# Instance norm with a gain, one core: from 32 units of 4 MB to 14 units of 8 MB between 4 small ones

## The chip, the core and the metric

The kernel runs on one core of one Trainium2 chip. The core has TensorE (PE) for matrix products, VectorE (DVE), ScalarE (ACT) and GpSimd (POOL) for elementwise work, SyncE (SP) that here only issues transfers, an on-chip memory (SBUF) of 128 partitions, and 16 DMA engines that move data between it and the device's memory (HBM). SP and ACT each feed a hardware queue of DMAs, in the profile q1 (SP) and q10 (ACT); POOL feeds q0. All three queues run on the same 16 engines.

The metric is the time of one execution on the device in microseconds (us). The kernel before took 627.33 us, the median of 3 runs (626.69 to 627.43).

## The reference

The input is x of shape 4 x 8 x 16 x 256 x 256 in 32-bit floats, which is 512 channels of 65,536 numbers (256 KB each, 134.2 MB in all), and gamma of 8 x 16 numbers. Each channel is normalized by its own mean and variance and scaled by the gamma of its place in the batch:

```python
mu = x.mean(axis=(3, 4), keepdims=True)
var = ((x - mu) ** 2).mean(axis=(3, 4), keepdims=True)
x_norm = (x - mu) / np.sqrt(var + 1e-5)
out = x_norm * gamma[None, :, :, None, None]
```

Every number has to be read once and written once: 134.2 MB each way.

## The kernel before

The 512 channels are cut into `U` = 32 units of 16 channels. A channel lies on `S` = 8 partitions with `F` = 8,192 numbers each, so that a unit fills 128 partitions with rows of 32 KB and is one contiguous piece of 4.19 MB in HBM. `AHEAD` = 6 slots (`xt0` to `xt5`, 192 KB of a partition together) take the units in turn; a unit is loaded into its slot, normalized in place and stored from there.

Before the loop, line 53 and 54 write a small zeroed tile `touch` to the output through POOL, line 55 loads gamma as one row, and six loads are issued (L48), units 1 and 3 through ACT's queue, the others through SP's. VectorE executes 60 instructions that do nothing. POOL makes `navg` (L67 to L72), a block matrix that holds -1/65536 where row and column belong to the same channel. Gamma's row is copied out eightfold into `g_rep` (L83), turned into columns by eight small matmuls (L88; 16 PE instructions in the profile, as each 32-bit matmul is two) and copied to `g_col` (L94): column n holds, on each partition, the gamma of the channel that lies there in unit n, n + 8 and so on.

The loop runs over the units, each engine in the order of the code:

- DVE sums the rows (L107), ACT squares them and sums the squares beside it (L108; its elementwise output `junk` is thrown away), into two columns of `st`.
- PE multiplies `st` by `navg` (L116). `ps` then holds, on all eight partitions of a channel, the negative mean and the negative mean of the squares.
- DVE makes the negative variance `nvar` (L117), ACT takes the root with 1e-5 added (L121), DVE the reciprocal (L125) and the product with gamma (L127).
- DVE subtracts the mean and multiplies, in place, over the whole tile (L130).
- ACT issues the store (L134), and SP issues the load of unit u + 6 into the same slot (L48), which waits until that store has landed.

What sets the order around the change are these two queues: SP's loads stand in line behind one another, each waiting for the store of the unit six before it; ACT's stores stand in line in its queue.

Of the kernel before, what the change touches and what calls it, by code (L numbers as in the profile page):

```python
# [1 line left out]

# [4 lines left out]

F32 = mybir.dt.float32
U8 = mybir.dt.uint8
ALU = mybir.AluOpType  # L10
ACTF = mybir.ActivationFunctionType
AX = mybir.AxisListType


@with_exitstack
def kernel(
    ctx: ExitStack,
    tc: tile.TileContext,
    x: bass.AP,
    gamma: bass.AP,  # L20
    out: bass.AP,
):
    nc = tc.nc
    B, G, C, H, W = x.shape
    P = nc.NUM_PARTITIONS
    HW = H * W
    n_ch = B * G * C
    S = 8
    K = P // S
    F = HW // S  # L30
    U = n_ch // K
    NG = (G * C) // K
    AHEAD = 6
    assert HW % S == 0 and (G * C) % K == 0

    xv = x.rearrange("b g c h w -> (b g c h w)").rearrange("(u p f) -> u p f", p=P, f=F)
    ov = out.rearrange("b g c h w -> (b g c h w)").rearrange("(u p f) -> u p f", p=P, f=F)
    gv = gamma.rearrange("g c -> (g c)")

    data = ctx.enter_context(tc.tile_pool(name="data", bufs=1))  # L40
    singles = ctx.enter_context(tc.tile_pool(name="singles", bufs=1))
    psum = ctx.enter_context(tc.tile_pool(name="psum", bufs=4, space=bass.MemoryType.PSUM))
    ctx.enter_context(tc.manual_schedule())

    slots = [data.tile([P, F], F32, name=f"xt{i}") for i in range(AHEAD)]

    def load(u, queue):
        queue.dma_start(out=slots[u % AHEAD][:], in_=xv[u])  # L48


    g_row = singles.tile([1, G * C], F32, name="g_row")
    touch = singles.tile([16, 128], F32, name="touch")
    nc.vector.memset(touch[:], 0.0)  # L53
    nc.gpsimd.dma_start(out=ov[0][0::S, 0:128], in_=touch[:])  # L54
    nc.gpsimd.dma_start(out=g_row[:], in_=gv[None, :])  # L55
    for u in range(AHEAD):
        load(u, nc.scalar if u in (1, 3) else nc.sync)

    for _ in range(60):
        nc.vector.nop()  # L60

    eps_t = singles.tile([P, 1], F32, name="eps_t")
    nc.gpsimd.memset(eps_t[:], 1e-5)
    one = singles.tile([1, 1], F32, name="one")
    nc.gpsimd.memset(one[:], 1.0)
    navg = singles.tile([P, K, S], F32, name="navg")
    nc.gpsimd.memset(navg[:], -1.0 / HW)  # L67
    nc.gpsimd.affine_select(  # L68
        out=navg[:], in_=navg[:], pattern=[[-S, K], [0, S]], compare_op=ALU.is_ge,
        fill=0.0, base=0, channel_multiplier=1,  # L70
    )
    nc.gpsimd.affine_select(  # L72
        out=navg[:], in_=navg[:], pattern=[[S, K], [0, S]], compare_op=ALU.is_ge,
        fill=0.0, base=S - 1, channel_multiplier=-1,
    )
    navg_w = navg[:].rearrange("p k s -> p (k s)")
    root_eps = singles.tile([P, 1], F32, name="root_eps")
    nc.scalar.activation(out=root_eps[:], in_=eps_t[:], func=ACTF.Sqrt)  # L78
    g_rep = singles.tile([1, NG, K, S], F32, name="g_rep")
    g_ps = psum.tile([P, NG], F32, name="g_ps", bufs=1)  # L80
    g_col = singles.tile([P, NG], F32, name="g_col")

    nc.vector.tensor_copy(  # L83
        out=g_rep[:],
        in_=g_row[:].rearrange("o (n k) -> o n k", n=NG).unsqueeze(3).to_broadcast([1, NG, K, S]),
    )
    for n in range(NG):
        nc.tensor.matmul(  # L88
            out=g_ps[:, n : n + 1],
            lhsT=g_rep[:, n].rearrange("o k s -> o (k s)"),  # L90
            rhs=one[:],
            start=True, stop=True,
        )
    nc.vector.tensor_copy(out=g_col[:], in_=g_ps[:])  # L94

    junk = singles.tile([P, F], U8, name="junk")

    st = singles.tile([P, U, 2], F32, name="st")
    nvar = singles.tile([P, U], F32, name="nvar")
    std = singles.tile([P, U], F32, name="std")  # L100
    rstd = singles.tile([P, U], F32, name="rstd")
    scale = singles.tile([P, U], F32, name="scale")

    squares = []
    for u in range(U):
        t = slots[u % AHEAD]
        nc.vector.reduce_sum(out=st[:, u, 0:1], in_=t[:], axis=AX.X)  # L107
        square = nc.scalar.activation(  # L108
            out=junk[:], in_=t[:], func=ACTF.Square, accum_out=st[:, u, 1:2],
        )  # L110
        if u:

            tc.declare_no_dep(square.ins, squares[-1].ins, reason="junk, ordered by the root between")
        squares.append(square)
        ps = psum.tile([P, 2], F32, name="ps")
        nc.tensor.matmul(out=ps[:], lhsT=navg_w, rhs=st[:, u], start=True, stop=True)  # L116
        nc.vector.tensor_scalar(  # L117
            out=nvar[:, u : u + 1], in0=ps[:, 0:1], scalar1=ps[:, 0:1],
            scalar2=ps[:, 1:2], op0=ALU.mult, op1=ALU.add,
        )  # L120
        nc.scalar.activation(  # L121
            out=std[:, u : u + 1], in_=nvar[:, u : u + 1], func=ACTF.Sqrt,
            bias=eps_t[:], scale=-1.0,
        )
        nc.vector.reciprocal(out=rstd[:, u : u + 1], in_=std[:, u : u + 1])  # L125
        g = u % NG
        nc.vector.tensor_mul(  # L127
            out=scale[:, u : u + 1], in0=rstd[:, u : u + 1], in1=g_col[:, g : g + 1],
        )
        nc.vector.tensor_scalar(  # L130
            out=t[:], in0=t[:], scalar1=ps[:, 0:1], scalar2=scale[:, u : u + 1],
            op0=ALU.add, op1=ALU.mult,
        )
        nc.scalar.dma_start(out=ov[u], in_=t[:])  # L134
        if u + AHEAD < U:
            load(u + AHEAD, nc.sync)


# [1 line left out]
_INS = ['x', 'gamma']  # L140
_OUTS = [((4, 8, 16, 256, 256), 'float32')]


# [23 lines left out]
```

## Time and profile before

| What | Value |
|---|---|
| median of 3 runs | 627.33 us (626.69 to 627.43) |
| span of the profiled execution | 625.8 us |
| DVE busy | 443.4 us, 71% |
| ACT busy | 238.8 us, 38% |
| HBM read, written | 134.22 MB, 134.23 MB |
| mean rate over the span | 429 GB/s |
| reduce of one unit (L107) | 8.684 us |
| squares of one unit (L108) | 7.030 us |
| multiply of one unit (L130) | 4.550 us |

The page of the profile gives for its own execution the span, from the first instruction to the last. Its part 2 cuts the span into 40 slices of 15.6 us and gives the busy share of each engine in tenths. The waits name who waited for whom; the chain follows the work that ended last back to its start; the issues list, for each transfer, the time from its issue to its landing. The trace also holds a record of each packet that a DMA engine moved, with its queue, start, duration and size. A few numbers are from these packet records, and the text says where.

### The profile page before, as it was taken

To read this page: it belongs to the slowest core of one execution; us is meant where nothing else is said; L and a number is where in the kernel's file an instruction comes from. 1 tells how busy PE (TensorE), PEld (TensorE's weight loads), DVE (VectorE), ACT (ScalarE), POOL (GpSimd) and SP (SyncE) were. 2 spreads that over 40 slices of the span, in tenths; PEclk is the share of its full clock that TensorE was granted. 3 is DMA by queue.
4 is the path that set the end of the run, shared out by engine and by line. 5 is a ranking of instruction groups with operands and counts; after the bars stand their busy time and mean duration, and the time that the engine had idled before them with its cause. 6 is when DMAs were issued, how large, how long until landed. Compare 5 with 4: busy or idle time off the path is not lost.

```text
span 625.8 us, 631 instructions
## 1 busy us (share of the span) xinstructions
PE 21.4 (3%) x80; PEld 19.5 (3%) x80; DVE 443.4 (71%) x163; ACT 238.8 (38%) x98; POOL 2.4 (0%) x11
## 2 busy tenths in 40 slices
PE   0200000000000000000000000000000000000000
PEld 0200000000000000000000000000000000000000
DVE  0588999999776687766776667867668676686730
ACT  0444444444443244432344423444224442244400
POOL 1000000000000000000000000000000000000000
DMA  8999999999999999999999999999999999999998
GB/s 369 436 415 429 429 436 436 436 436 434 424 434 434 434 436 434 431 429 434 436 436 436 436 431 427 431 436 431 436 434 434 429 434 436 436 436 436 429 425 354
DMA packets 9282, 268.46 MB, mean 429 GB/s; under 512 B 1072, under 2 KB 1088, under 8 KB 1088
## 3 DMA queue, kind: packets, MB, share of 16 engines
q10 hardware_dynamic: 4896, 142.61, 52.9%
q1 hardware_dynamic: 4320, 125.83, 46.7%
q0 software_dynamic: 64, 0.01, 0.0%
q14 instruction: 2, 0.02, 0.0%
HBM read 134.22 MB, written 134.23 MB: 429 GB/s over the span
## 4 chain that ended last, share of the span: by engine, by line
another core or an unknown queue 61%; DMA 17%; DVE 15%; SPq 1%; PE 1%; issue 0%; ACT 0%
DVE st L107 10%; DMA xt<-in_x_dram 10%; DMA out_dram<-xt 8%; DVE xt L130 5%; SPq L48 1%; PE ps L116 1%; ACT std L121 0%; DVE nvar L117 0%; DVE rstd L125 0%; DVE scale L127 0%
## 5 line engine op out<-in xcount | busy, mean ns | idle before, releaser
L107 DVE TENSOR_REDUCE st<-xt 128x1 f32<-128x8192 f32 x32 | 277.9, 8684 | 101.2 <-DMA xt<-in_x_dram 101.2
L108 ACT ACTIVATE junk<-xt 128x8192 uint8<-128x8192 f32 x32 | 225.0, 7030 | 276.0 <-DMA xt<-in_x_dram 232.8
L130 DVE TENSOR_SCALAR xt<-xt,ps,scale 128x8192 f32<-128x8192 f32 x32 | 145.6, 4550 | 1.2
L121 ACT ACTIVATE std<-nvar,eps_t 128x1 f32<-128x1 f32 x32 | 9.4, 294 | 79.6 <-DVE nvar L117 79.6
L116 PE MATMUL ps<-st,navg 128*128 128x2 f32 x64 | 17.9, 349 | 558.0 <-DVE st L107 558.0
L116 PEld LDWEIGHTS ps<-st,navg 128*128 128x128 f32 x64 | 16.0, 311 | 559.8 <-issue 559.8
L117 DVE TENSOR_SCALAR nvar<-ps 128x1 f32<-128x1 f32 x32 | 9.2, 287 | 23.8 <-PE ps L116 23.8
L125 DVE RECIPROCAL rstd<-std 128x1 f32<-128x1 f32 x32 | 5.2, 164 | 11.6 <-ACT std L121 11.6
L83 DVE COPY g_rep<-g_row 1x1024 f32<-1x1024 f32 x1 | 0.7, 680 | 14.3 <-DMA g_row<-in_gamma_dram 14.3
L108 ACT ACTIVATION_READ_ACCUMULATOR junk<-xt 128x1 f32 x32 | 6.0, 187 | 0.0
L127 DVE TENSOR_TENSOR scale<-rstd,g_col 128x1 f32<-128x1 f32 x32 | 5.1, 159 | 1.1
L88 PE MATMUL g_ps<-one,g_rep 1*128 1x1 f32 x16 | 3.5, 346 | 16.2 <-DVE g_rep L83 16.2
L88 PEld LDWEIGHTS g_ps<-one,g_rep 1*128 1x128 f32 x16 | 3.5, 325 | 16.1 <-issue 16.1
L94 DVE COPY g_col<-g_ps 128x8 f32<-128x8 f32 x1 | 0.2, 166 | 3.7 <-PE g_ps L88 3.7
L78 ACT ACT_TABLE_LOAD x1 | 1.3, 1283 | 1.7 <-PEq L151 1.7
L53 DVE MEMSET touch<- 16x128 f32 x1 | 0.2, 165 | 0.9 <-PEq L151 0.9
L54 POOL DMA_DIRECT2D out_dram<-touch x1 | 0.6, 619 | 0.8 <-DVE touch L53 0.8
L55 POOL DMA_DIRECT2D g_row<-in_gamma_dram x1 | 0.5, 487 | 0.0
L68 POOL TENSOR_SCALAR_AFFINE_SELECT navg<-navg 128x128 f32<-128x128 f32 x1 | 0.4, 400 | 0.1
L72 POOL TENSOR_SCALAR_AFFINE_SELECT navg<-navg 128x128 f32<-128x128 f32 x1 | 0.4, 399 | 0.1
L67 POOL MEMSET navg<- 128x128 f32 x1 | 0.2, 232 | 0.0
L78 ACT ACTIVATE root_eps<-eps_t 128x1 f32<-128x1 f32 x1 | 0.2, 202 | 0.0
(6 smaller groups left out, 0.6 us busy)
## 6 DMA issues: line engine op xcount, KB each, us to landing
out_dram<-xt ACTq DMA_DIRECT2D x32, 4096.0 KB, 62.5
xt<-in_x_dram SPq DMA_DIRECT2D x30, 4096.0 KB, 38.5
xt<-in_x_dram ACTq DMA_DIRECT2D x2, 4096.0 KB, 31.6
out_dram<-touch POOLq DMA_DIRECT2D x1, 8.0 KB, 9.1
g_row<-in_gamma_dram POOLq DMA_DIRECT2D x1, 0.5 KB, 13.3
```

Of the source, the lines that this page charges most:

```text
L48: queue.dma_start(out=slots[u % AHEAD][:], in_=xv[u])
L78: nc.scalar.activation(out=root_eps[:], in_=eps_t[:], func=ACTF.Sqrt)
L83: nc.vector.tensor_copy(out=g_rep[:], in_=g_row[:].rearrange("o (n k) -> o n k", n=NG).unsqueeze(3).to_broadcast([1, NG, K, S]),)
L88: nc.tensor.matmul(out=g_ps[:, n : n + 1], lhsT=g_rep[:, n].rearrange("o k s -> o (k s)"), rhs=one[:], start=True, stop=True,)
L107: nc.vector.reduce_sum(out=st[:, u, 0:1], in_=t[:], axis=AX.X)
L108: square = nc.scalar.activation(out=junk[:], in_=t[:], func=ACTF.Square, accum_out=st[:, u, 1:2],)
L116: nc.tensor.matmul(out=ps[:], lhsT=navg_w, rhs=st[:, u], start=True, stop=True)
L117: nc.vector.tensor_scalar(out=nvar[:, u : u + 1], in0=ps[:, 0:1], scalar1=ps[:, 0:1], scalar2=ps[:, 1:2], op0=ALU.mult, op1=ALU.add,)
L121: nc.scalar.activation(out=std[:, u : u + 1], in_=nvar[:, u : u + 1], func=ACTF.Sqrt, bias=eps_t[:], scale=-1.0,)
L125: nc.vector.reciprocal(out=rstd[:, u : u + 1], in_=std[:, u : u + 1])
L127: nc.vector.tensor_mul(out=scale[:, u : u + 1], in0=rstd[:, u : u + 1], in1=g_col[:, g : g + 1],)
L130: nc.vector.tensor_scalar(out=t[:], in0=t[:], scalar1=ps[:, 0:1], scalar2=scale[:, u : u + 1], op0=ALU.add, op1=ALU.mult,)
```

## The change

Units now come in two sizes. The first two and the last two are as before (16 channels on 8 partitions each, 4.19 MB). The 28 units between are joined to 14 of 32 channels on 4 partitions each, with rows of 64 KB, 8.39 MB a unit. There are three slots of 64 KB a partition, so that the slots take the same 192 KB. Units 0 and 1 share slot 0, one half each, and so do the last two, 16 and 17; units 2 to 15 take the slots 1, 2, 0 in turn.

- A large unit is summed by one instruction and squared by two, of 8,192 numbers each, as `junk` keeps its size; `st` has three columns for it. PE multiplies all three at once. `nvar` takes in the first half's squares, and a new instruction makes the bias `rest` of the root from the second half's.
- There are two block matrices, `navg8` and `navg4`, by a new function `blocks`.
- Gamma is loaded as a tile of 32 partitions x 4 numbers and turned into columns by three matmuls with 0/1 matrices (`pick8a`, `pick8b`, `pick4`), also made by `blocks`. `gamma_of` picks the column of a unit.
- The `touch` write and the 60 idle instructions of DVE are gone. All loads go through SP's queue: four before the loop (units 0 to 3), unit 4 after unit 1, then in the turn of unit u the load of unit u + 3. In the turn of unit 13 the loads of 16 and 17 are issued; in the turn of unit 14, u + 3 is 17, and the load of unit 17 is issued there as well. The program built from it has 19 loads and 18 stores on the two hardware queues. The last load waits for the one before it, into the same bytes, and unit 17's reduce and squares wait for the last.

The core of the diff:

```diff
-    S = 8
-    K = P // S
-    F = HW // S
-    U = n_ch // K
-    NG = (G * C) // K
-    AHEAD = 6
+    GC = G * C
+    SLOTS = 3
+    FS = HW // 8
+    FB = HW // 4
+    KB, KS = P // 4, P // 8
...
-    slots = [data.tile([P, F], F32, name=f"xt{i}") for i in range(AHEAD)]
+    slots = [data.tile([P, FB], F32, name=f"xt{i}") for i in range(SLOTS)]
+    units = []
+    first = 0
+    turn = 0
+    def small(pair):
+        nonlocal first, turn
+        for h in range(2):
+            units.append((first, 8, slots[turn % SLOTS][:, h * FS : (h + 1) * FS]))
+            first += KS
+        turn += 1
+    small(0)
+    while first < n_ch - KB:
+        units.append((first, 4, slots[turn % SLOTS][:]))
+        first += KB
+        turn += 1
+    small(1)
+    U = len(units)
...
+    def load(u):
+        nc.sync.dma_start(out=units[u][2], in_=rows(flat_x, u))
...
-    touch = singles.tile([16, 128], F32, name="touch")
-    nc.vector.memset(touch[:], 0.0)
-    nc.gpsimd.dma_start(out=ov[0][0::S, 0:128], in_=touch[:])
-    nc.gpsimd.dma_start(out=g_row[:], in_=gv[None, :])
-    for u in range(AHEAD):
-        load(u, nc.scalar if u in (1, 3) else nc.sync)
-    for _ in range(60):
-        nc.vector.nop()
+    for u in range(4):
+        load(u)
+    with nc.allow_non_contiguous_dma(reason="128 numbers"):
+        nc.gpsimd.dma_start(out=g_kn[:], in_=gamma.rearrange("g c -> (g c)").rearrange("(n k) -> k n", k=KB))
...
+    def blocks(name, rows_, k, s, value, base):
+        t = singles.tile([rows_, k, P // k], F32, name=name)
+        nc.gpsimd.memset(t[:], value)
+        nc.gpsimd.affine_select(
+            out=t[:], in_=t[:], pattern=[[-s, k], [0, P // k]], compare_op=ALU.is_ge,
+            fill=0.0, base=-base, channel_multiplier=1,
+        )
+        nc.gpsimd.affine_select(
+            out=t[:], in_=t[:], pattern=[[s, k], [0, P // k]], compare_op=ALU.is_ge,
+            fill=0.0, base=s - 1 + base, channel_multiplier=-1,
+        )
+        return t[:].rearrange("p k s -> p (k s)")
+    navg = {8: blocks("navg8", P, KS, 8, -1.0 / HW, 0), 4: blocks("navg4", P, KB, 4, -1.0 / HW, 0)}
...
+    for i in range(3):
+        nc.tensor.matmul(out=g_ps[:, i], lhsT=pick[i], rhs=g_kn[:], start=True, stop=True)
     nc.vector.tensor_copy(out=g_col[:], in_=g_ps[:])
...
     for u in range(U):
...
+        for h in range(parts):
+            square = nc.scalar.activation(
+                out=junk[:], in_=t[:, h * FS : (h + 1) * FS], func=ACTF.Square,
+                accum_out=st[:, u, 1 + h : 2 + h],
+            )
...
+        bias = eps_t[:]
+        if parts == 2:
+            bias = rest[:, u : u + 1]
+            nc.vector.tensor_scalar(
+                out=bias, in0=ps[:, 2:3], scalar1=-1.0, scalar2=1e-5, op0=ALU.mult, op1=ALU.add,
+            )
...
-        nc.scalar.dma_start(out=ov[u], in_=t[:])
-        if u + AHEAD < U:
-            load(u + AHEAD, nc.sync)
+        nc.scalar.dma_start(out=rows(flat_o, u), in_=t)
+        if u == 1:
+            load(4)
+        elif 2 <= u and u + 3 < U:
+            load(u + 3)
+            if u + 3 == U - 2:
+                load(U - 1)
```

## The prediction

> **What bounds the kernel now.** I read the page's slices first, then its queues and DMA issues, the windows, the waits of SP's queue and the chain. The slices show DMA engines that are never free, beside a DVE that idles 29% of the span:
>
> ```profile
> span 625.8 us, 631 instructions
> PE 21.4 (3%) x80; PEld 19.5 (3%) x80; DVE 443.4 (71%) x163; ACT 238.8 (38%) x98; POOL 2.4 (0%) x11
> DMA  8999999999999999999999999999999999999998
> q10 hardware_dynamic: 4896, 142.61, 52.9%
> q1 hardware_dynamic: 4320, 125.83, 46.7%
> ```
>
> The queues carry 34 + 30 = 64 transfers of 4.19 MB, each of 128 rows of 32 KB (and 16 completion packets). What one costs is in the windows (last column GB/s):
>
> ```profile
> 200.00:300.00 100.00, 2.78 (x10) 2.50 (x10) 72.53 (x26) 40.38 (x16) 0.00 (x0) 1.00 1.00 433
> 300.00:400.00 100.00, 2.80 (x10) 2.51 (x10) 72.42 (x26) 39.89 (x17) 0.00 (x0) 1.00 1.00 433
> ```
>
> 4.19 MB at 433 GB/s is 9.68 us: I call this one transfer. 64 of them are 619.6, and the first data move 1.8 into the span (packet records), so an even stream would end at 621.4; the span is 4.4 longer (slower first packets, engines that end up to 1.3 apart, the last landing). I carry these 4.4 over. The median of the runs (627.33) is 1.5 above the profiled span; I carry that too.
>
> SP's waits (in total, times, longest) say that loads wait for stores to free their slot, so the transfers feed each other:
>
> ```profile
> SPq L48 <- DMA out_dram<-xt: 535.3, 26, 59.6
> ```
>
> What covers the last unit is seen in the chain (start, duration) and in the issues (last column: us to landing):
>
> ```profile
> 547.61 38.49 DMA xt<-in_x_dram
> 586.12 8.70 DVE st L107
> 594.95 0.57 PE ps L116 x2
> 596.59 4.55 DVE xt L130
> ```
>
> ```profile
> out_dram<-xt ACTq DMA_DIRECT2D x32, 4096.0 KB, 62.5
> xt<-in_x_dram SPq DMA_DIRECT2D x30, 4096.0 KB, 38.5
> out_dram<-touch POOLq DMA_DIRECT2D x1, 8.0 KB, 9.1
> g_row<-in_gamma_dram POOLq DMA_DIRECT2D x1, 0.5 KB, 13.3
> ```
>
> The last load lands at 586.1 and its unit is ready 15.0 later, at 601.1. The span ends at 625.8, because stores wait 62.5 us in ACT's queue: four of them (38.7 us) are still to move when the last load ends. So the 15 us of arithmetic cost nothing. The small POOL rows show how queues share an engine: 512 bytes of gamma take 13.3 us. By the packet records each small packet starts 2.43 us after the one before it, the time of two 32 KB rows (1.213 each): a row is not cut, and each queue gets one packet per turn, whatever its size.
>
> **The change, part by part.**
>
> *Traffic.* Reading the loop's last lines: at u = 13, `load(16)` is followed by `load(U - 1)`, that is 17; at u = 14 the condition `u + 3 < U` still holds, and `load(17)` is issued again. So there are 19 loads (5 of 4.19 MB, 14 of 8.39) for 18 stores: 33 transfers read, 32 written, 65 in all. One more costs 9.68 us on engines that have no free time. It waits on SP until the first load of 17 has landed (same bytes); nothing is queued behind it there, but unit 17's reduce and squares wait for it.
>
> *Joined DMAs.* 56 of the 64 transfers become 28, SP and ACT issue fewer. An issue takes 0.33 us on a queue that runs ahead: nothing either way. A 64 KB row could cost as much as two 32 KB rows (2 x 1.213) or save one packet's fixed part; nearest row for that part is a 4-byte completion packet, 9 ns: 4 packets x 56 x 9 ns = 2.0 us gained at most. I take 0, since eight rows at 1.213 already make a transfer, and keep 2.0 for the range. The Trainium skill (DMA: Bandwidth & Descriptors, Anatomy of one DMA) puts a DMA at 2.0 us plus bytes at 436 GB/s; 28 fixed parts less would be an estimated 56 us saved if they stood in line. This trace has no such part: a transfer every 9.68 us, queued behind one another.
>
> *Units of 8 MB.* Reduce 2 x 8.68, matmul 0.57, `nvar` 0.30, the new `rest` about 0.3 (as `nvar`, one column), root 0.30, reciprocal and product 0.34, multiply 2 x 4.55, gaps 0.3: 28.5 us, against a pair of 8.39 MB transfers in 38.7. ACT's two squares, 2 x 7.2, end before the reduce does. 18 units take fewer small instructions than 32, but DVE is not what is waited for: 0.
>
> *Three slots.* A slot must go round in 3 x 38.7 = 116.2 us. Its needs: load 38.7 and store 38.7 (both sharing), 28.5, and some 4.3 for starts and landings (1.0 from issue to data, 1.55 from the last data of a load to DVE's start, 0.7 for a store to SP): 110.2. It fits with 6 to spare, and if it did not, the other queue would take the whole rate: DMA stands still only when all three slots are in arithmetic. 0 in the steady part. But the backlog of stores in ACT's queue shrinks from three or four transfers to one being written, and that was the cover of the end.
>
> *Head.* All first loads now go through SP, 25 MB back to back until 60 us, as before. The 128 single numbers of gamma are 8 packets an engine and a completion, one turn each: against one queue of 32 KB rows 9 x 1.21 = 10.9 after a start at about 6, so 17 us; `g_col`'s copy stands before unit 0's reduce on DVE, which so starts near 18 and not at 13. Unit 2 lands near 48 and finds DVE free by 48: 0. If a turn is 2.4, gamma lands near 30 and one or two gaps of 1.7 to 2.6 us open near 80 and 120: 5 us is the upper end. POOL's fifteen small instructions for the five matrices (0.23 to 0.40 each) end near 8 us. The pauses on DVE, the `touch` DMA and the sixteen gamma matmuls (3.5 us) all lay under the first load (22.6): 0.
>
> *The end, which decides.* I play the schedule forward from these rows, one packet per queue and turn. Load 15 ends its data near 546.5, store 14 having begun 5 us before. The small loads 16, 17, 17 again have rows of 32 KB, the stores 14 and 15 rows of 64 KB: a load gets a third of the engine. Load 16 ends near 573 (store 14 done at 571.6). Load 17 runs alone until unit 15 is stored from 577.6, then at a third: 592.6 to 597. Its repeat starts some 2.6 later (landing, issue), at a third against store 15, evenly against store 16 (32 KB rows): 618 to 620. Stores 15 and 16 end at 621.4. Then nothing is left to move: 1.55 landing, 15.0 arithmetic, 1.0 to the first packet, and only at 635.6 to 637.6 does store 17 begin. DMA idles 14 to 16 us.
>
> Sum: 635.6 to 637.6 + 9.68 = 645.3 to 647.3; + 4.4 = 649.7 to 651.7 span; + 1.5 = 651.2 to 653.2. I say **652.0**, that is 9.7 for the repeated load and about 15 for the uncovered end.
>
> **Rivals.**
> *Even shares.* If a 64 KB row is carried as two packets, or engines share by bytes, loads get a half: load 17 ends near 585, its repeat near 607, with 14 us of stores left to cover the 17.6 of landing, arithmetic and start. The idle time is 3.2 us: 624.6 + 9.68 + 4.4 + 1.5 = 640.2. For it: the trace has no row over 32 KB. Against it: a 4-byte packet waited a full turn of two rows.
>
> *64 KB rows move worse.* Neighbouring rows in HBM stand 64 KB apart and not 32. The nearest row of a lower rate is the window 20:40, reads alone: 423 GB/s against 433. Were the 56 joined transfers slower by that 2.3%, 12.5 us more, 664.5. No row has such a pitch, and the first packets had other reasons to be slow. The Trainium skill (DMA: Bandwidth & Descriptors, Latency and other measured facts) speaks against the change here: a row pitch of 512 KiB gave 207 GB/s a direction where 214 is full, 2 MiB 164; 64 KB is below its smallest, and no run here shows any of it. By that 3.3% the estimate would be 18 us more.
>
> *Not slower.* The mechanism would be in the steady part: long rows moving faster. To pay for 25 us, the 56 joined transfers would have to take 9.24 us and not 9.68, 454 GB/s. The bound above is 2.0 us; packets already follow each other with no gap (eight of 1.213 are 9.70). It would also be no slower if the repeat were not issued at all; then by the same schedule 64 transfers and 0 to 3 us without work, 627 to 630, no change or hardly one. The code issues it.
>
> **How the numbers follow.** By turns 0.70 (646 to 658), even shares 0.17 (636 to 645), slower rows 0.08 (658 to 670), not slower 0.05. The range takes the first and nearly all of the second: 638 to 658, about 0.83. Its likeliest part is 647 to 657. About 0.2% (1.3 us) is what a measurement of this kernel can tell from no change. Faster 0.03, same 0.02, slower 0.95.
>
> **What would show it.** 19 loads beside 18 stores, 137 MB read or more (138.4 against 134.2); a DMA digit that drops to 0 once, in the last but one or two slices, for 14 to 16 us (3 with even shares); a last load issued near 594 to 598 that lands near 620 (608); unit 17's reduce starting there, and a chain that ends in load, reduce, multiply, store; 433 GB/s in the middle. Wrong would be: gaps in the middle (three slots too few), another rate in 200:500 (row size matters), or a first unit on DVE after 30 us with holes near 80.

## The result, and the profile after

The changed kernel takes 653.3 us (652.8 to 655.1, 4 runs) against 627.4 of the kernel before: ratio 1.0423, 95% interval 1.0407 to 1.0438, 25.9 us slower. 652.0 was forecast. The profiled execution has a span of 651.6 us, 1.8 below its own time of 653.4. Runs more than 1.5% above the fastest run of their kernel are left out of all ratios.

The page after, its first part, slices, queues and traffic:

```profile
span 651.6 us, 434 instructions
PE 11.5 (2%) x42; PEld 10.4 (2%) x42; DVE 429.4 (66%) x105; ACT 234.7 (36%) x84; POOL 6.2 (1%) x21
DMA  8999999999999999999999999999999999999926
...
q1 hardware_dynamic: 2736, 138.41, 49.4%
q10 hardware_dynamic: 2592, 134.22, 47.6%
...
HBM read 138.41 MB, written 134.22 MB: 418 GB/s over the span
```

The 434 instructions are some two thirds of 631, and this bought nothing: at 66% busy, DVE is not what bounds the kernel. 138.41 MB read are 4.19 more than the input has, the second load of unit 17. And the DMA row, nines until then, has a hole in its last two slices. The windows show how wide it is, and that the middle is as it was (last column GB/s):

```profile
300.00:400.00 100.00, 1.12 (x4) 1.01 (x4) 65.48 (x14) 33.86 (x11) 0.00 (x0) 1.00 1.00 435
400.00:500.00 100.00, 1.67 (x6) 1.50 (x6) 74.92 (x18) 38.84 (x15) 0.00 (x0) 1.00 1.00 435
600.00:620.00 20.00, 0.00 (x0) 0.00 (x0) 0.00 (x0) 0.00 (x0) 0.00 (x0) 1.00 1.01 429
626.00:640.00 14.00, 0.56 (x2) 0.50 (x2) 12.27 (x5) 5.84 (x3) 0.00 (x0) 1.00 0.00 0
```

From 626 to 640 the DMA engines start nothing, while one unit goes through DVE. The end of the chain (start, duration) tells why:

```profile
545.90 53.68 another core or an unknown queue
599.58 0.02 issue
599.60 24.80 DMA xt<-in_x_dram
624.40 0.02 issue
624.42 8.70 DVE st L128
...
634.89 4.55 DVE xt L159
```

SP waits 53.68 us for the first load of unit 17. The chain does not know it by name; SP's waits do:

```profile
SPq L70 <- DMA xt<-in_x_dram: 53.7, 1, 53.7
```

The repeat is issued at 599.6 and lands at 624.4. The last packet of the stores before it ends at 626.5, by the packet records, and store 17 is issued at 639.48 and starts to move at 640.32: 13.8 us in which no data move. In the kernel before, the last unit went through the same 15 us of arithmetic (586.1 to 601.2) while the three stores ahead of its own were moving, until 614.4 by the packet records.

### The profile page after: what moved, and what is told of

The parts are those of the page before. It is cut to its first block, busy times and chain, and to the rows that moved or that the text cites. A ratio compares the mean times of both kernels' runs of the same rounds, so it can differ in the third digit from the quotient of the medians.

```text
span 651.6 us, 434 instructions
## 1 busy us (share of the span) xinstructions
PE 11.5 (2%) x42; PEld 10.4 (2%) x42; DVE 429.4 (66%) x105; ACT 234.7 (36%) x84; POOL 6.2 (1%) x21
## 3 DMA queue, kind: packets, MB, share of 16 engines
q1 hardware_dynamic: 2736, 138.41, 49.4%
HBM read 138.41 MB, written 134.22 MB: 418 GB/s over the span
## 4 chain that ended last, share of the span: by engine, by line
DMA 65%; DVE 23%; another core or an unknown queue 8%; PE 1%; issue 0%; ACT 0%; SPq 0%
DMA out_dram<-xt 33%; DMA xt<-in_x_dram 32%; DVE st L128 15%; DVE xt L159 8%; PE ps L138 1%; ACT std L151 0%; DVE nvar L141 0%; DVE rstd L155 0%; DVE scale L156 0%; SPq L70 0%; DVE rest L148 0%
## 5 line engine op out<-in xcount | busy, mean ns | idle before, releaser
L128 DVE TENSOR_REDUCE st<-xt 128x1 f32<-128x16384 f32 (+1 forms) x18 | 275.8, 15323 | 177.9 <-DMA xt<-in_x_dram 177.9
L159 DVE TENSOR_SCALAR xt<-xt,ps,scale 128x16384 f32<-128x16384 f32 (+1 forms) x18 | 141.7, 7870 | 0.7
L151 ACT ACTIVATE std<-nvar,rest 128x1 f32<-128x1 f32 x14 | 4.1, 295 | 57.1 <-DVE rest L148 57.1
L138 PE MATMUL ps<-st,navg 128*128 128x3 f32 (+1 forms) x36 | 10.1, 350 | 612.8 <-DVE st L128 612.8
L138 PEld LDWEIGHTS ps<-st,navg 128*128 128x128 f32 x36 | 9.0, 312 | 613.8 <-issue 613.8
L141 DVE TENSOR_SCALAR nvar<-ps 128x1 f32<-128x1 f32 x18 | 5.2, 288 | 13.4 <-PE ps L138 13.4
L155 DVE RECIPROCAL rstd<-std 128x1 f32<-128x1 f32 x18 | 2.9, 164 | 6.5 <-ACT std L151 6.5
L151 ACT ACTIVATE std<-nvar,eps_t 128x1 f32<-128x1 f32 x4 | 1.2, 294 | 9.5 <-DVE nvar L141 9.5
L156 DVE TENSOR_TENSOR scale<-rstd,g_col 128x1 f32<-128x1 f32 x18 | 2.9, 159 | 0.6
L148 DVE TENSOR_SCALAR rest<-ps 128x1 f32<-128x1 f32 x14 | 2.1, 148 | 0.0
```

The costliest lines, as they stand in the source:

```text
L128: nc.vector.reduce_sum(out=st[:, u, 0:1], in_=t, axis=AX.X)
L138: nc.tensor.matmul(out=ps[:, : 1 + parts], lhsT=navg[s], rhs=st[:, u, : 1 + parts], start=True, stop=True,)
L141: nc.vector.tensor_scalar(out=nvar[:, u : u + 1], in0=ps[:, 0:1], scalar1=ps[:, 0:1], scalar2=ps[:, 1:2], op0=ALU.mult, op1=ALU.add,)
L148: nc.vector.tensor_scalar(out=bias, in0=ps[:, 2:3], scalar1=-1.0, scalar2=1e-5, op0=ALU.mult, op1=ALU.add,)
L151: nc.scalar.activation(out=std[:, u : u + 1], in_=nvar[:, u : u + 1], func=ACTF.Sqrt, bias=bias, scale=-1.0,)
L156: nc.vector.tensor_mul(out=scale[:, u : u + 1], in0=rstd[:, u : u + 1], in1=gamma_of(u),)
```

## The experiments

**One load.** Only the condition is changed:

```diff
-        elif 2 <= u and u + 3 < U:
+        elif 2 <= u and u + 3 < U - 1:
```

> The changed kernel with unit 17 loaded once, nothing else changed. Theory (the repeat and the end it uncovers cost the 26 us, the joined units themselves nothing): 64 transfers again. Load 17 lands at 599.6 as in the changed kernel, its unit is ready at 614.6, stores 15 and 16 last until about 616.8, so the end is covered: span 627 to 629, 628.5 to 630.5 us in all, 0 to 3 above the kernel before. Rival (three slots or rows of 64 KB cost time in the middle): it stays above 640.

Measured: 629.4 us against 627.2 of the kernel before on the same chip, ratio 1.0035 (1.0022 to 1.0048). So some 24 of the 26 us (25.9 - 2.2) hang on the second load, and the joined units, three slots, long rows, gamma's new matmuls and the new head cost 2.2 us together. The timeline of its end:

```profile
597.28 8.69 DVE L128 TENSOR_REDUCE st<-xt 128x1 f32<-128x8192 f32 x1 [3.09 <-DMA xt<-in_x_dram]
612.34 0.34 ACTq L163 DMA_DIRECT2D out_dram<-xt  x1
```

Unit 17 is ready at 612.3; the stores before it end at 614.5 by the packet records. It is covered, by 2 us. The 2.2 us that are left lie within the 0 to 3 that the prediction had for this case. In the profiled executions most of them are at the very end: the packets of the last store start at 613.2 here and in the kernel before, and end at 625.9 here and at 624.5 there, because a few of the 16 engines are behind the others (most end at 623.0).

**The kernel before with a repeat.** Its last load is issued twice:

```diff
         if u + AHEAD < U:
             load(u + AHEAD, nc.sync)
+            if u + AHEAD == U - 1:
+                load(u + AHEAD, nc.sync)
```

> The kernel before with its last unit loaded a second time after the first load has landed, nothing else changed. Theory: the repeat is issued at 586 with four stores (39 us) still to move, shares evenly with them, lands near 607, its unit is ready near 622, while stores last until 625: covered, so only the transfer itself is paid, 9.7 us: 637 (636 to 639). Rival (a repeat costs its 25 us wherever it stands, since the unit waits for it): 648 to 653.

Measured: 637.7, 10.5 more than the kernel before (ratio 1.0172, 1.0155 to 1.0189). The same repeat, waited for in the same way, costs 10.5 us here and 23.9 (653.3 - 629.4) in the changed kernel. Its timeline shows what the difference is:

```profile
585.46 0.33 SPq L48 DMA_DIRECT2D xt<-in_x_dram  x1
608.46 8.69 DVE L107 TENSOR_REDUCE st<-xt 128x1 f32<-128x8192 f32 x1 [27.35 <-DMA xt<-in_x_dram]
623.51 0.34 ACTq L134 DMA_DIRECT2D out_dram<-xt  x1
```

DVE idles 27 us for the repeat, and that costs almost nothing, because the store before ends only at 623.8 and the last one starts at 624.4: 0.5 us without data. What is paid is the transfer, and little more.

**Short rows at the end.** The repeat stays; the stores of units 14 and 15 are cut into halves:

```diff
-        nc.scalar.dma_start(out=rows(flat_o, u), in_=t)
+        if u in (14, 15):
+            for h in range(2):
+                half = slice(h * FS, (h + 1) * FS)
+                nc.scalar.dma_start(out=rows(flat_o, u)[:, half], in_=t[:, half])
+        else:
+            nc.scalar.dma_start(out=rows(flat_o, u), in_=t)
```

> The changed kernel, repeat and all, with the stores of units 14 and 15 cut into two of 32 KB rows each. Theory (a queue gets one packet a turn, whatever its size): the small loads now get half and not a third of the engines. Load 17 lands near 587 to 590, the repeat near 608 to 612, DMA idles 3 to 6 us and not 14: 640 to 644. Rival (shares go by bytes, rows don't matter): no change, 653.

Measured: 640.8, ratio 1.0216 to the kernel before, and 12.5 below the changed kernel, with the same bytes, the same units and one store DMA more for each of the two. The timeline:

```profile
588.05 0.33 SPq L70 DMA_DIRECT2D xt<-in_x_dram  x1
611.32 8.69 DVE L128 TENSOR_REDUCE st<-xt 128x1 f32<-128x8192 f32 x1 [19.67 <-DMA xt<-in_x_dram]
```

The first load of 17 lands at 588 and not 599.6, the repeat at 611 and not 624.4, and the stores before store 17 end at 624.7 by the packet records (626.5 in the changed kernel). So DMA idles 2.6 us (624.7 to 627.2, a little under the 3 to 6 expected) and not 13.8. Only the length of a row in the *other* queue was changed, and the packet records show what that does to the shares. Beside store 14, load 16 moved 2.73 MB while the store moved 5.83 in the changed kernel (551 to 571 us): a third. With short rows it moved 2.21 beside 2.13 (550 to 560): half.

**The repeat put aside.** Unit 17 is loaded once, and the second load goes into a free half of slot 1, where no one waits for it:

```diff
-        elif 2 <= u and u + 3 < U:
+        elif 2 <= u and u + 3 < U - 1:
...
+        if u == 14:
+            nc.sync.dma_start(out=slots[1][:, 0:FS], in_=rows(flat_x, U - 1))
```

> The changed kernel with its second load of unit 17 put into the half of slot 1 that is free by then, so that no one waits for it; the same 65 transfers. Theory: the traffic costs 9.7 and the waiting unit the rest. Unit 17 is ready near 615, the end is covered, 9.7 above the kernel before: 637 to 640. Rival (the extra traffic itself costs 25, by disturbing the queues): 650 or more.

Measured: 643.4 (641.8 to 644.2), 3.4 above the expected end. That misses the theory's range, though it is far below the rival's 650. Not waiting gained 10 us and not the whole 13.8. Its windows:

```profile
615.00:620.00 5.00, 0.00 (x0) 0.00 (x0) 2.01 (x1) 0.00 (x0) 0.00 (x0) 1.00 1.03 446
620.00:625.00 5.00, 0.00 (x0) 0.00 (x0) 0.00 (x0) 0.00 (x0) 0.00 (x0) 1.00 1.03 446
625.00:630.00 5.00, 0.00 (x0) 0.00 (x0) 0.00 (x0) 0.00 (x0) 0.00 (x0) 1.00 1.00 433
630.00:640.00 10.00, 0.00 (x0) 0.00 (x0) 0.00 (x0) 0.00 (x0) 0.00 (x0) 1.00 0.36 157
```

There is no hole, but a long tail: after 630 only a part of the engines still works. In the packet records one engine's packets follow each other end to start, so that the 16 can be told apart. Those of the last store reach from 622.1 to 640.5, 18.4 us where eight rows of 1.21 are 9.7; ten engines end by 632.4 and six between 636.6 and 640.5. The load of unit 17, which had the extra load behind it in SP's queue and not ahead of it, was done on the first engine at 583.6 and on the last at 601.6, and unit 17 was summed from 602.0. The engines had come apart, and a DMA lands with its slowest engine.

**Aside, with short rows.** The two edits before in one kernel, to see whether the rows did that.

> The changed kernel with its second load of unit 17 put into the free half of slot 1, as before, and the stores of units 14 and 15 in rows of 32 KB. With long rows this took 643.4, 3.4 above what one more transfer explains. Theory (engines drift apart where a 64 KB row stands beside a 32 KB row, and the load waits for the slowest engine): 637 to 639. Rival (the extra load delays unit 17 by its turn in the queue, rows don't matter): 642 to 644.

Measured: 637.7 (ratio 1.0165, 1.0150 to 1.0180), 10.8 above the kernel before, as after the repeat in that one. The timeline shows unit 17 summed from 592.2, directly behind unit 16, and its packet records the load of unit 17 done between 586.0 and 588.2 on all engines and the last store in 12.9 us:

```profile
592.24 8.68 DVE L128 TENSOR_REDUCE st<-xt 128x1 f32<-128x8192 f32 x1
607.30 0.34 ACTq L168 DMA_DIRECT2D out_dram<-xt  x1
```

So the 5.7 us between this kernel and that of the last experiment come from the 64 KB rows of these two stores beside 32 KB rows, partly by the load's smaller share and, as the packet records suggest, by engines that come apart.

**One load and short rows at the end.** The edits of the first and the third experiment together.

> The changed kernel with unit 17 loaded once and the stores of units 14 and 15 in rows of 32 KB, two DMAs each. With one load alone the last store's packets reached from 613.25 to 625.92, 12.7 us, where the kernel before has 11.3. Theory (rows of two sizes beside one another let the engines drift apart at the end, and this is the 2 us that are left): 627.0 to 628.3, no change against the kernel before. Rival (the 2 us come from large rows or units anywhere else): 629 to 630, as with one load alone.

Measured: 628.0 against 626.9 as medians. But the twelve runs reach from 627.4 to 641.3 with five of them at 629.3 or more, where the 29 runs of the kernel before stay between 626.7 and 627.6. The ratio of 1.0027 (1.0010 to 1.0044), which is without the longest run, stands for 1.7 us. The one trace is of that longest run, and its windows show a lower rate long before the end:

```profile
300.00:400.00 100.00, 1.68 (x6) 1.50 (x6) 64.78 (x18) 29.38 (x11) 0.00 (x0) 1.00 1.00 422
400.00:500.00 100.00, 1.12 (x4) 1.00 (x4) 69.35 (x13) 43.34 (x14) 0.00 (x0) 1.00 1.00 417
```

By the packet records 162 of the 1,280 packets of 64 KB that start in these windows took more than 2.45 us, up to 4.3; in the changed kernel's trace it was 5 of 1,327. Why they were slow in that run is open.

**All rows short.** One load, and each load and store of a large unit cut into two DMAs of 32 KB rows:

```diff
     def load(u):
-        nc.sync.dma_start(out=units[u][2], in_=rows(flat_x, u))
+        for h in range(8 // units[u][1]):
+            half = slice(h * FS, (h + 1) * FS)
+            nc.sync.dma_start(out=units[u][2][:, half], in_=rows(flat_x, u)[:, half])
...
-        nc.scalar.dma_start(out=rows(flat_o, u), in_=t)
+        for h in range(parts):
+            half = slice(h * FS, (h + 1) * FS)
+            nc.scalar.dma_start(out=rows(flat_o, u)[:, half], in_=t[:, half])
```

> The changed kernel with unit 17 loaded once and every load and store of the large units cut into two DMAs of 32 KB rows; units, slots and instructions on the engines stay joined. A load's first half now also waits only for the first half of the store. Theory (joined units cost nothing, rows of 64 KB cost the last 2 us): 626.8 to 628.2. Rival (three slots cost them): 629 to 630.

Here a load's first half also waits only for the first half of the store, so more than the rows was changed. Measured: 627.9 against 626.9 as medians, with one of eleven runs at 636.0; ratio 1.0024 (1.0003 to 1.0046), which stands for 1.5 us. The medians of this kernel and of the one before it lie where the theory put them, 1.0 and 1.1 above the kernel before and not 2.2. But the three intervals (with the first experiment's 1.0022 to 1.0048) overlap, and neither of these two is clear of 1 by much. That long rows cost about one of the last 2 us fits, and is not shown.

**The head alone.** The kernel before without the `touch` write and VectorE's idle instructions, and with all six first loads on SP:

```diff
-    touch = singles.tile([16, 128], F32, name="touch")
-    nc.vector.memset(touch[:], 0.0)
-    nc.gpsimd.dma_start(out=ov[0][0::S, 0:128], in_=touch[:])
...
-        load(u, nc.scalar if u in (1, 3) else nc.sync)
+        load(u, nc.sync)
...
-    for _ in range(60):
-        nc.vector.nop()
```

> The kernel before with the changed kernel's head alone: no touch write, no idle instructions on VectorE, all six first loads through SP's queue. Theory (all this lies under the first loads): 626.8 to 628.0, no change. Rival (the touch write or the second queue at the start saves time): 629 or more; (they cost time): 626 or less.

Measured: 627.5 against 626.9, ratio 1.0007 (0.9998 to 1.0015). No change that can be told. Its unit 0 starts at 12.9 and not at 22.6, now that no second queue moves data beside its load; the total does not notice.

No version tried beats the kernel before: the medians of the four with 64 transfers all lie within 0.4% of it.

## Why the prediction was right

*What bounds the kernel.* Right: 435 GB/s from 300 to 500 after and 433 before, with 434 instructions or 631.

*The sum.* 9.7 for the repeat, 13.8 without data and the 2.2 that are left with one load make 25.7 of the 25.9 us. The last of these three had no term: the joined DMAs, the three slots, the larger units and the head were all put at 0.

*Traffic, 9.7 us.* Right. The load put aside, with short rows, costs 9.7 over the same kernel without it (637.7 against 628.0, by the medians). In the kernel before, the repeat costs 10.5, of which 0.5 is the time without data before the last store; 0.3 is not accounted for.

*The uncovered end, 14 to 16 us.* Right in mechanism, and 0.2 under the range: 13.8 us without data. With the end covered (one load) or with even shares (short rows) it shrinks to nothing or to 2.6. The schedule behind it was right in its order and late in its times: the data of load 17 end at 596.8 (592.6 to 597 was forecast), the repeat starts to move 6.9 later (2.6) and its data end at 623.2 (618 to 620), the stores before store 17 end at 626.5 (621.4), and store 17 starts at 640.3 (635.6 to 637.6).

The term that was too small is the time between one load and the next. From the last data of load 17 to its landing it was 2.8 us and not 1.55: the completion packet waits its turn behind a row of the other queue, here a longer one. From issue to the first packet, 1.0 was right where the engines stand idle (0.84 for store 17), but where the other queue keeps them busy it took 3.3 (store 15) and 4.1 (the repeat), and also 3.4 and 3.5 in the two kernels where that queue had 32 KB rows (the repeat in the kernel before, and short rows at the end).

Two errors nearly cancelled, and that the total came within 1.3 us is partly luck. Store 17 began 2.7 to 4.7 us late. But of the 4.4 us that the forecast added behind its transfer, only 1.7 came there (651.65 less 640.32 and 9.68). The time of load 17 is luck in part, too. Eleven engines were done with it between 588.2 and 591.3, earlier than forecast, as store 15 began late. Five had begun it up to 2.9 us behind the first and were done between 595.7 and 599.2, as each of their rows that was left when store 15 came cost a turn of 3.6 us. The forecast had all engines alike.

*Shares by turns.* Right, and the disputed part of the forecast: the even-shares rival stood at 640.2, and the kernel that was made to share evenly took 640.8. The packet records after show why: the 64 KB rows are single packets of 2.418 us, twice 1.213 less 8 ns, and on each engine they alternate one by one with the load's 32 KB rows.

*Joined DMAs, 0 with 2.0 us as the bound of a gain.* No gain is seen in the time, nor a loss by row pitch in the middle: the windows 300:400 and 400:500 give 435 GB/s after and 433 before. The figures on row pitch of the Trainium skill (DMA: Bandwidth & Descriptors, Latency and other measured facts) begin at 512 KiB; at 64 KB these windows show no loss. The fixed part of 2.0 us a DMA (the Trainium skill, DMA: Bandwidth & Descriptors, Anatomy of one DMA), which the page gives for DMAs that POOL issues, is not paid here by DMAs that queue behind one another on SP's and ACT's queues.

*Units of 8 MB, 28.5 us.* 27.9 (549.72 to 577.65 for unit 15). The new `rest` takes 0.148 and not 0.3. No effect.

*Head.* Wrong in a number that had no effect. Gamma was to land near 17 and unit 0 to start near 18. Gamma landed 8.1 us after its issue, near 9.5, and unit 0 started when its load landed, at 14.4. The assumption that failed is one packet for each of the 128 numbers: the packet records have one of 32 bytes for each engine, and a completion. The two gaps near 80 and 120 that a late gamma could have opened are not there.

## What to carry to other kernels

Where the DMA engines never idle, fewer and larger instructions bought nothing here, and the things to count are bytes and what still waits in the store queue when the last load lands: that backlog is what hides the last unit's arithmetic. Read the loop's last turns with their numbers: a condition that still holds one turn after a special case has issued the same load costs its traffic and, worse, its wait. And queues that share an engine take turns by packet: beside a queue of 64 KB rows, one of 32 KB rows got a third here. An engine that is behind when the long rows come falls further behind: 2.9 us became 11 in the changed kernel.

## What the runs showed of the hardware that was not expected

- Cutting the rows of one queue's stores from 64 KB to 32 KB made the loads of the other queue land 11.6 us earlier (588.0 and not 599.6) and the kernel 12.5 us faster.
- In kernels with rows of 64 KB the engines can come apart. The packets of the last 4 MB store reach over 18.4 us with the load put aside, over 12.9 with that and short rows at the end, and over 12.7 with one load. In the kernels of 32 KB rows alone they reach over 11.3 (before), 10.9 (the head alone) and 10.6 (all rows short). Single 64 KB packets took up to 3.6 us with the load put aside and not 2.418. Each of these is one execution, and why some engines fall behind was not tried.
- From issue to the first packet, a DMA with its own queue empty took 0.84 us where the engines stood idle and 3.3 to 4.1 us where the other queue kept them busy.
- 128 numbers of 4 bytes, read with a stride by POOL's queue, travelled as 16 packets of 32 bytes.
